# Weight splits issued ahead of other ready work on ScalarE and VectorE

## The chip, the cores and the metric

The kernel runs on one core of a Trainium2 chip. The metric is the device time of one execution in microseconds (us). Before the change the median of three runs is 1501.51 us (1500.48 to 1504.97).

## The reference, cut to what matters

A two-layer block (mixer A, convolutional FFN, mixer B, convolutional FFN, final norm) is followed by a block with a second mixer and a mixture of 32 experts. There are 256 tokens of width 1024, all in float32.

```python
for i in range(2):                       # first block
    x = x + (mixer_a if i == 0 else mixer_b)(rms_norm(x), ...)
    x = x + conv_ffn(rms_norm(x), ...)
h = rms_norm(x)                          # second block
proj = (rmsnorm(h) * (1 + sc1) + sh1) @ w_in          # 1024 -> q, kv, index, rwkv, 2 gates
o_attn = sparse_attention(q, k, v, index)             # 8 heads of 64
o_rwkv = rwkv7_time_mix(p_shift, ...)                 # 8 heads of 64, a recurrence over time
merged = sigmoid(gate_a) * (o_attn @ w_branch_attn) + sigmoid(gate_r) * (o_rwkv @ w_branch_rwkv)
h = h + gt1 * (merged @ w_out)
h = h + gt2 * moe(rmsnorm(h))            # top 2 of 32 experts, SwiGLU, 1024 -> 512 -> 1024
```

## The kernel before, in words

**Products of three.** Outside the experts every product of a weight matrix is made of three matmuls (`mm3`, L267 to L274): high part by high part (L272), and the two cross products (L273, L274). So each operand must be split in a high part in the fp32r format and a low part. `split_act` (L303 to L306) does it: ScalarE copies to the high part (L305), VectorE subtracts it from the source (L306). Activations are split by it too, and in other places by L366 (ScalarE) and L367 (VectorE) straight out of a transpose.

**The stream of weights.** `wload` (L244) takes a piece of 128 x 1024 weights: it issues the load on SyncE's queue (`load_raw`, L241) into a ring of raw places, and splits the piece into one of four split places, the tiles arena_r_78 to arena_r_81 in the orders below. A split place is free again when the last matmul that reads it is done, and a raw place when its split is done.

**Stages.** TensorE goes through mixer A, FFN, mixer B, FFN, final norms, the second mixer, the router, and the experts. In the second mixer the projections run first (`rwkv_prep` L967, `rwkv_pairs` L1038, `qkv` L1275, `gate` L1414). Eight gate groups of 48 matmuls each are spread over what follows. The RWKV recurrence (`rwkv_chain`, L1102) is a chain of small steps: it inverts a matrix (L1077 to L1087), writes it to memory and reads it back in another layout (L1090, L1128, both issued by ScalarE), and then goes through L1137, L1143, L1145, L1153, L1157 four times, and through L1167, L1173, L1178, L1187 four times. Between any two of these matmuls ScalarE or VectorE evacuates the result. After it comes `rwkv_out` (L1194, a group norm, transposes L1209, and a split). The attention goes in four parts: scores L1344, softmax on VectorE and ScalarE (L1346 to L1359), transposes L1364, product with the values L1370, split. `branch` (L1421) then multiplies attention by w_branch_attn and RWKV by w_branch_rwkv, and `second_mixer` (L1433) ends with w_out. In the orders below, pg_8110 to pg_9223 are the gates, pg_9291 to pg_9369 the attention branch, and pg_9410 and pg_9439 the RWKV branch.

**Experts.** `expert_pass` (L1668) streams 32 experts of 6 MB through places of 1 MB, loaded at L1665 on SyncE's queue. Twenty places are loaded ahead while the second mixer runs; every other load waits until a place is read by an expert matmul (L1709, L1735).

**What sets the order.** The program is handed to a scheduler that orders the instructions of each engine. Among instructions that it takes as ready it picks by priority, which without a mark is the place in the program. The engines then run their instructions in the order written, each waiting for its semaphores.

Of the kernel before, what the change touches and what calls it, by code (L numbers as in the profile page):

```python
# [90 lines left out]
def view(v, dims, dtype):  # L91
    if dtype not in (F32, F32R):
        v = v.bitcast(dtype)
    names = "abcde"[:len(dims)]
    if len(dims) > 1:
        left = f"({' '.join(names)})"
        v = v.rearrange(f"p {left} -> p {' '.join(names)}", **dict(zip(names, dims)))
    return v
# [8 lines left out]
class Net:  # L107
# [108 lines left out]
        return t  # L216


    PIECE, WPIECE = 1024, 2048

    def ring(self, raw, split):

# [21 lines left out]
    def wload(self, src):  # L244

        a, b = src.shape[1], src.shape[2]
        step = self.PIECE // b
        assert -(-a // step) <= len(self.places["split"][0])
        out = []
        for a0 in range(0, a, step):  # L250
            m = min(step, a - a0)
            raw = self.load_raw(src[:, a0:a0 + m])
            o = self.place("split")
            parts = [view(self.ar.cols(o + i * self.PIECE, m * b), (m, b), F32R) for i in range(2)]
            self.split_act(parts[0], parts[1], raw)
            out += [(parts[0][:, i], parts[1][:, i]) for i in range(m)]
        return out

# [1528 lines left out]
```

## Time and profile before

| what | before |
|---|---|
| median of 3 runs | 1501.51 us |
| the profiled execution | 1502.12 us |
| its span, first to last instruction | 1500.4 us |
| mean granted TensorE clock | 0.950 |
| TensorE busy | 1371.2 us |
| VectorE busy | 852.7 us |
| ScalarE busy | 615.2 us |

The span leaves 1.7 us of the profiled execution outside it, and the profiled execution lies 0.6 us over the median. A time in the rows is counted from the span's start. A matmul's duration is modelled and overlaps with the next one; the distance from start to start tells the pace.

### The profile page before, as it was taken

The page shows a single profiled execution, that of the slowest core. Times are in us where ns is not written, and L with a number is a line of the kernel's source. Part 1 is how long each engine was busy: PE and PEld are TensorE (multiplying, and loading weights), DVE is VectorE, ACT ScalarE, POOL GpSimd, SP SyncE. Part 2 cuts the span into 40 slices and gives each one's busy share as a digit, 9 for nine tenths or more (in the row PEclk, how much of TensorE's full clock was granted, in tenths as well). Part 3 has the DMA queues.
Part 4 walks back from the last instruction along what each step waited for, and adds up shares of the span by engine and source line. Part 5 has one row for each costly group of instructions (what it writes and reads, how often), then busy time and mean ns, then how long its engine had stood idle before and what let it go on. Part 6 is the DMA issues. An engine that isn't in the chain of part 4 may idle for free.

```text
span 1500.4 us, 22885 instructions
## 1 busy us (share of the span) xinstructions
PE 1371.2 (91%) x9085; PEld 1042.1 (69%) x9085; DVE 852.7 (57%) x1628; ACT 615.2 (41%) x955; POOL 32.2 (2%) x63
## 2 busy tenths in 40 slices
PE   7999999999999899999999899998978878879785
PEld 6778999999998689999798688887413313234131
DVE  5796798778788789878859742775201101101011
ACT  6644555556688555555575544552100000000000
POOL 3000000000001000000000100001000000000000
PEclk9999999999999999999899795999999989999998
DMA  9898586555555578563243352487999999999997
GB/s 318 282 327 277 158 274 215 187 187 160 170 182 184 172 272 275 187 191 109 72 153 113 99 121 86 170 336 308 390 421 420 420 420 421 421 421 419 421 419 253
DMA packets 165573, 391.18 MB, mean 261 GB/s; under 512 B 19440, under 2 KB 101100, under 8 KB 141780
## 3 DMA queue, kind: packets, MB, share of 16 engines
q1 hardware_dynamic: 153124, 383.64, 70.2%
q10 hardware_dynamic: 11136, 4.53, 1.3%
q0 software_dynamic: 1200, 1.49, 0.4%
q8 instruction: 73, 1.20, 0.3%
q14 instruction: 40, 0.33, 0.1%
HBM read 386.19 MB, written 3.43 MB: 260 GB/s over the span
## 4 chain that ended last, share of the span: by engine, by line
PE 58%; DMA 29%; DVE 7%; ACT 4%; issue 2%; SPq 0%; POOL 0%; DVEq 0%; ACTq 0%
DMA arena<-expert_w_gate 12%; PE ps L272 9%; PE ps L273 9%; PE ps L274 9%; DMA arena_w<-expert_w_gate 7%; DMA arena_w<-expert_w_down 6%; PE pc L273 5%; PE pc L272 5%; PE pc L274 5%; DMA arena<-expert_w_down 3%; PE pg L272 2%; PE pg L274 2%; PE pg L273 2%; DVE arena_r L306 2%; ACT arena_r L305 1%
## 5 line engine op out<-in xcount | busy, mean ns | idle before, releaser
L305 ACT ACTIVATE arena_r<-arena 128x1024 fp32r<-128x1024 f32 (+2 forms) x330 | 328.9, 1008 | 287.1 <-PE ps L273 73.1
L306 DVE TENSOR_TENSOR arena_r<-arena,arena_r 128x1024 fp32r<-128x1024 f32 (+2 forms) x330 | 376.9, 1154 | 119.2 <-ACT arena_r L305 115.8
L272 PE MATMUL ps<-arena_r,arena_r 128*128 128x256 f32 (+2 forms) x1192 | 353.7, 297 | 1.0 <-DVE arena L818 1.0
L273 PE MATMUL ps<-arena_r,arena_r 128*128 128x256 f32 (+2 forms) x1192 | 352.9, 296 | 1.1 <-DVE arena_r L306 1.1
L274 PE MATMUL ps<-arena_r,arena_r 128*128 128x256 f32 (+2 forms) x1192 | 352.4, 296 | 0.6 <-DVE arena_r L306 0.6
L272 PEld LDWEIGHTS ps<-arena_r,arena_r 128*128 128x128 f32 (+1 forms) x1192 | 229.3, 192 | 10.4 <-issue 3.5
L273 PEld LDWEIGHTS ps<-arena_r,arena_r 128*128 128x128 f32 (+1 forms) x1192 | 229.2, 192 | 7.2 <-DVE arena_r L306 1.5
L274 PEld LDWEIGHTS ps<-arena_r,arena_r 128*128 128x128 f32 (+1 forms) x1192 | 229.2, 192 | 5.6 <-DVE arena_r L306 0.8
L1709 PE MATMUL pc<-arena 128*32 128x512 f32 x576 | 144.4, 672 | 34.1 <-DMA arena<-expert_w_up 18.9
L272 PE MATMUL pc<-arena_r,arena_r 128*128 128x512 f32 x344 | 136.0, 399 | 5.3 <-ACT arena_r L305 3.4
L273 PE MATMUL pc<-arena_r,arena_r 128*128 128x512 f32 x344 | 135.9, 395 | 0.4 <-DVE arena_r L306 0.4
L274 PE MATMUL pc<-arena_r,arena_r 128*128 128x512 f32 x344 | 134.2, 393 | 0.0
L1709 PE MATMUL pc<-arena_w,arena 128*32 128x512 f32 x448 | 117.4, 663 | 15.8 <-DMA arena_w<-expert_w_gate 9.8
L1716 DVE TENSOR_TENSOR arena<-arena,pc 128x512 f32<-128x512 f32 x8 | 5.5, 688 | 204.6 <-PE pc L1709 204.6
L1692 ACT ACTIVATE arena<-ps,mod_col,moe_g 128x128 f32<-128x128 f32 x32 | 14.7, 458 | 246.1 <-DVE arena L1694 246.1
L1709 PEld LDWEIGHTS pc<-arena 128*32 128x32 f32 x576 | 31.4, 120 | 99.1 <-issue 37.1
L272 PE MATMUL pg<-arena_r,arena_r 128*128 128x256 f32 (+1 forms) x312 | 95.0, 306 | 2.0 <-DVE arena L916 1.8
L273 PE MATMUL pg<-arena_r,arena_r 128*128 128x256 f32 (+1 forms) x312 | 94.7, 305 | 1.1 <-DVE arena_r L306 1.1
L274 PE MATMUL pg<-arena_r,arena_r 128*128 128x256 f32 (+1 forms) x312 | 95.1, 306 | 0.2 <-DVE arena_r L306 0.2
L521 DVE SCALAR_TENSOR_TENSOR arena<-arena 128x255 f32<-128x255 f32 (+2 forms) x228 | 94.4, 477 | 0.2
L1735 PE MATMUL pc<-arena 128*32 128x512 f32 (+2 forms) x320 | 74.7, 584 | 11.5 <-DMA arena<-expert_w_down 7.6
L272 PEld LDWEIGHTS pc<-arena_r,arena_r 128*128 128x128 f32 x344 | 65.2, 190 | 19.8 <-ACT arena_r L305 5.1
(451 smaller groups left out, 1688.2 us busy)
## 6 DMA issues: line engine op xcount, KB each, us to landing
arena<-f_w_up SPq DMA_DIRECT2D x96, 512.0 KB, 3.9
arena<-expert_w_gate SPq DMA_DIRECT2D x41, 1024.0 KB, 19.9
arena<-expert_w_down SPq DMA_DIRECT2D x34, 1024.0 KB, 19.9
arena_w<-expert_w_up SPq DMA_DIRECT2D x33, 1024.0 KB, 19.9
arena<-expert_w_up SPq DMA_DIRECT2D x31, 1024.0 KB, 19.9
arena_w<-expert_w_down SPq DMA_DIRECT2D x26, 1024.0 KB, 19.9
arena<-ada_w SPq DMA_DIRECT2D x48, 512.0 KB, 5.6
arena<-f_w_down SPq DMA_DIRECT2D x48, 512.0 KB, 4.2
```

The source lines that it names most:

```text
L272: nc.tensor.matmul(acc, ah, bh, start=first, stop=False, **kw)
L273: nc.tensor.matmul(acc, ah, bl, start=False, stop=False, **kw)
L274: nc.tensor.matmul(acc, al, bh, start=False, stop=last, **kw)
L305: self.nc.scalar.activation(hi, src, AF.Copy)
L306: self.nc.vector.tensor_tensor(lo, src, hi.bitcast(F32), ALU.subtract)
L521: nc.vector.scalar_tensor_tensor(o[:, i:], src[:, :S - i], w[k - 1 - i], o[:, i:], op0=ALU.mult, op1=ALU.add)
L1692: nc.scalar.activation(xg[:, k], ps[:, j], AF.Identity, scale=g, bias=sh)
L1709: nc.tensor.matmul(gu[i][es], xg[:, kk, es], ws[e][:, k], start=kk == 0, stop=kk == 7, skip_group_check=True)
L1716: tt(hd, hd, gu[1], ALU.mult)
L1735: nc.tensor.matmul(o[es], hT[:, k0 + k, es], ws[e][:, k, f0 - c0:f0 - c0 + n], start=k0 + k == 0, stop=k0 + k == 3, skip_group_check=True)
```

## The change

The weight split inside `wload` is put under a raised priority of 3000; the splits of activations that call `split_act` elsewhere stay as they were. Loads, sizes, places and results are the same.

```diff
-    PIECE, WPIECE = 1024, 2048
+    PIECE, WPIECE, URGENT = 1024, 2048, 3000
...
             parts = [view(self.ar.cols(o + i * self.PIECE, m * b), (m, b), F32R) for i in range(2)]
-            self.split_act(parts[0], parts[1], raw)
+            with self.tc.high_priority(self.URGENT):
+                self.split_act(parts[0], parts[1], raw)
             out += [(parts[0][:, i], parts[1][:, i]) for i in range(m)]
```

The orders of ScalarE, VectorE, TensorE and SyncE differ after it. In the changed file every line from L255 on has a number higher by one, so L305 is L306 there, L366 is L367, and so on; the texts use the numbers of before.

ScalarE at the start of the kernel, before. L366 writes the normalized activations of the first layer, L305 the weights.

```order
L305 ACTIVATE arena_r_79<-arena 128x1024
L305 ACTIVATE arena_r_80<-arena 128x1024
L366 ACTIVATE arena_r_76<-ps_95,g_a 128x256
L366 ACTIVATE arena_r_76<-ps_96,g_a 128x256
L305 ACTIVATE arena_r_81<-arena 128x1024
L366 ACTIVATE arena_r_76<-ps_119,g_a 128x256
L366 ACTIVATE arena_r_76<-ps_95,g_a 128x256
L366 ACTIVATE arena_r_76<-ps_120,g_a 128x256
L366 ACTIVATE arena_r_76<-ps_96,g_a 128x256
L366 ACTIVATE arena_r_76<-ps_119,g_a 128x256
L305 ACTIVATE arena_r_78<-arena 128x1024
```

The same place on ScalarE, now:

```order
L306 ACTIVATE arena_r_79<-arena 128x1024
L306 ACTIVATE arena_r_80<-arena 128x1024
L306 ACTIVATE arena_r_81<-arena 128x1024
L367 ACTIVATE arena_r_76<-ps_95,g_a 128x256
L367 ACTIVATE arena_r_76<-ps_96,g_a 128x256
L306 ACTIVATE arena_r_78<-arena 128x1024
L367 ACTIVATE arena_r_76<-ps_119,g_a 128x256
L367 ACTIVATE arena_r_76<-ps_120,g_a 128x256
L367 ACTIVATE arena_r_76<-ps_95,g_a 128x256
L335 ACTIVATE ps_193,ss_10_194<-arena 128x512
L306 ACTIVATE arena_r_79<-arena 128x1024
L367 ACTIVATE arena_r_76<-ps_96,g_a 128x256
```

The third weight piece now stands ahead of the first activations, and the fourth and fifth ahead of most of the rest.

TensorE in the second mixer, where the first of the chain's four rounds ends and the second runs, before. Small shapes are the chain, L1344 and L1364 the attention, pg_9055 the fifth gate group.

```order
L1153 MATMUL pc_8405<-arena 32x32 x8
L1157 MATMUL pc_8415<-arena 32x32 x8
L1137 MATMUL pc_8425<-arena 32x16 x16
L1143 MATMUL pc_8443<-arena 16x16 x16
L1145 MATMUL pc_8443<-arena 32x16 x8
L272 MATMUL pg_9055<-arena_r_76,arena_r_79 128x256
L273 MATMUL pg_9055<-arena_r_77,arena_r_79 128x256
L1153 MATMUL pc_8471<-arena 32x32 x8
L1364 MATMUL ps_8913<-ident,arena 128x128 x3
```

The same place on TensorE, now:

```order
L274 MATMUL pg_9111<-arena_r_77,arena_r_78 128x256
L275 MATMUL pg_9111<-arena_r_76,arena_r_78 128x256
L1154 MATMUL pc_8405<-arena 32x32 x8
L1158 MATMUL pc_8415<-arena 32x32 x8
L1138 MATMUL pc_8425<-arena 32x16 x16
L1144 MATMUL pc_8443<-arena 16x16 x16
L1146 MATMUL pc_8443<-arena 32x16 x8
L273 MATMUL pg_9167<-arena_r_76,arena_r_79 128x256
L274 MATMUL pg_9167<-arena_r_77,arena_r_79 128x256
```

Between the first round's L1145 and its L1153 there now stand the rest of gate group 9055 and the whole of 9111, and the filler inside the chain is group 9167, which stood behind the chain before. Over the whole chain, from the first L1137 to the last L1187, there are 98 of the products of three (single matmuls) before and 197 now; between the last L1187 and the first matmul of the RWKV branch there are 190 before and 72 now.

TensorE around the last L1187 (the chain's end), before:

```order
L272 MATMUL pg_9167<-arena_r_76,arena_r_79 128x256
L273 MATMUL pg_9167<-arena_r_77,arena_r_79 128x256
L1187 MATMUL pc_8780<-arena 64x64 x8
L274 MATMUL pg_9167<-arena_r_76,arena_r_79 128x256
L272 MATMUL pg_9167<-arena_r_76,arena_r_79 128x256
```

And now:

```order
L1188 MATMUL pc_8780<-arena 64x64 x8
L1210 MATMUL pc_8839<-ident,arena 128x128 x2
L1365 MATMUL ps_8995<-ident,arena 128x128
L1210 MATMUL pc_8839<-ident,arena 128x128
L1365 MATMUL ps_8995<-ident,arena 128x128 x2
L1365 MATMUL ps_9000<-ident,arena 128x128 x3
L1371 MATMUL ps_9005<-arena 64x128
L1345 MATMUL ps_9014<-arena 128x128
L1371 MATMUL ps_9005<-arena 64x128 x5
L1345 MATMUL ps_9015<-arena 128x128
L1345 MATMUL ps_9014<-arena 128x256
L1345 MATMUL ps_9015<-arena 128x256
```

What followed the chain before was 94 matmuls of the last two gate groups; now the transposes of `rwkv_out` and the third and fourth parts of the attention follow it directly, with 24 matmuls of the attention branch among them.

## Rows read from the trace of the kernel before

**Rows 1.** Busy time, windows of the span; columns are named in the answer's head.
```profile
0.00:1050.00 1050.00, 1010.07 (x7203) 904.28 (x7207) 792.12 (x1513) 594.37 (x911) 32.23 (x63) 0.96 0.61 199
90.00:420.00 330.00, 329.98 (x2208) 301.88 (x2208) 266.55 (x415) 189.18 (x259) 0.00 (x0) 1.00 0.66 212
1050.00:1495.00 445.00, 361.13 (x1890) 137.80 (x1882) 60.63 (x117) 20.88 (x44) 0.00 (x0) 0.94 1.00 408
```

**Rows 2.** Waits of SyncE's DMA queue, 1000 to 1060 us.
```profile
SPq L1665 <- PE pc L1709: 23.2, 3, 19.1
```

**Rows 3.** Timeline of TensorE where the experts begin; start, us, what.
```profile
1047.76 4.06 PE L1709 MATMUL pc<-arena 128*32 128x512 f32 x34
```

**Rows 4.** Waits of TensorE, 0 to 1050 us: total, times, longest us.
```profile
PE pc L272 <- ACT arena_r L305: 3.4, 2, 1.7
PE pg L273 <- DVE arena_r L306: 1.1, 1, 1.1
...
PE pg L274 <- DVE arena_r L306: 0.2, 1, 0.2
```

**Rows 5.** Timeline of TensorE, 486 to 496 us: the two waits for L305.
```profile
486.73 0.49 PE L272 MATMUL pc<-arena_r,arena_r 128*128 128x512 f32 x1 [1.71 <-ACT arena_r L305]
...
495.07 0.50 PE L272 MATMUL pc<-arena_r,arena_r 128*128 128x512 f32 x1 [1.67 <-ACT arena_r L305]
```

**Rows 6.** Timeline of ScalarE, the same stretch.
```profile
486.05 0.63 ACT L305 ACTIVATE arena_r<-arena 128x512 fp32r<-128x512 f32 x1 [0.68 <-DVE arena L643]
...
494.40 0.62 ACT L305 ACTIVATE arena_r<-arena 128x512 fp32r<-128x512 f32 x1
```

**Rows 7.** Timeline of ScalarE, start of the kernel.
```profile
10.40 1.06 ACT L305 ACTIVATE arena_r<-arena 128x1024 fp32r<-128x1024 f32 x1 [0.66 <-DMA arena<-a_w_in]
11.37 0.82 ACT L366 ACTIVATE arena_r<-ps,g_a 128x256 fp32r<-128x256 f32 x2
12.08 1.06 ACT L305 ACTIVATE arena_r<-arena 128x1024 fp32r<-128x1024 f32 x1
```

**Rows 8.** Timeline of TensorE, its first product.
```profile
11.87 0.79 PE L272 MATMUL pc<-arena_r,arena_r 128*128 128x512 f32 x1 [1.89 <-ACT arena_r L366]
```

**Rows 9.** Timeline of TensorE, the RWKV chain and what follows it.
```profile
891.34 0.68 PE L1137 MATMUL pc<-arena 32*32 32x16 f32 x32
...
897.24 0.90 PE L1157 MATMUL pc<-arena 32*32 32x32 f32 x13 [1.87 <-ACT arena L1154]
...
958.65 1.14 PE L1187 MATMUL pc<-arena 64*64 64x64 f32 x16
...
969.41 0.92 PE L1344 MATMUL ps<-arena 64*128 64x128 f32 x4
...
980.02 0.27 PE L1364 MATMUL ps<-ident,arena 128*128 128x128 f32 x1
...
991.76 0.28 PE L273 MATMUL pg<-arena_r,arena_r 128*128 128x256 f32 x1
991.88 0.28 PE L274 MATMUL pg<-arena_r,arena_r 128*128 128x256 f32 x1
```

**Rows 10.** Timeline of VectorE, split of the last attention part.
```profile
984.03 0.42 DVE L306 TENSOR_TENSOR arena_r<-ps,arena_r 128x256 fp32r<-128x256 f32 x1 [1.39 <-ACT arena_r L305]
```

**Rows 11.** Windows ahead of and in the chain; third number from the end: granted clock.
```profile
830.00:840.00 10.00, 5.94 (x33) 4.40 (x34) 9.77 (x16) 7.71 (x13) 0.00 (x0) 0.91 0.59 180
840.00:850.00 10.00, 8.58 (x50) 7.99 (x47) 7.37 (x22) 6.04 (x11) 3.45 (x6) 0.50 0.17 54
...
897.00:934.00 37.00, 36.15 (x483) 30.89 (x483) 10.47 (x17) 17.57 (x46) 0.00 (x0) 0.50 0.28 86
934.00:958.00 24.00, 24.00 (x315) 20.90 (x313) 12.79 (x24) 10.49 (x19) 0.00 (x0) 1.00 0.16 48
```

**Rows 12.** Timeline of ScalarE, between the two memory trips of the RWKV chain.
```profile
870.73 5.22 ACTq L1090 DMA_DIRECT2D x_img<-arena  x8
876.28 0.60 ACT L1419 ACTIVATE arena<-pg 128x512 f32<-128x512 f32 x1 [8.00 <-DMA x_img<-arena]
```

## The prediction

> **What bounds the kernel now.** The windows of busy time come first, because they show two regimes. Up to 1050 us TensorE is busy 1010.07 of 1050.00 us; in 90 to 420 us it is busy 329.98 of 330.00 us at full clock. From 1050 us on the DMA share is 1.00 at 408 GB/s while TensorE has 361.13 busy of 445.00 us [rows 1]. So the second regime is a fixed stream of expert weights. It begins when TensorE begins the experts: the loads made ahead have filled every place, and SyncE's queue waits up to 19.1 us for the first expert matmuls to free one [rows 2], which start at 1047.76 us [rows 3]. The end therefore follows this start one for one when it comes later. A start some us earlier passes on too, as long as the loads ahead are in. What the change is worth is TensorE's idle time, plus time lost to a half clock, before 1047.76 us. Idle time there is 1050.00 - 1010.07 = 39.9 us in all [rows 1].
>
> The second view is what ends TensorE's waits. The change can only shorten directly those that end on a weight split. On L305 there are two, 3.4 us together; on L306 there are five, from 1.1 down to 0.2 us, which make 3.4 us [rows 4]. That would be 6.8 us, but the two on L305 stand at 486.73 and 495.07 us [rows 5], and the ScalarE instructions that finish just ahead of them are 128x512 pieces at 486.05 and 494.40 us, the first itself waiting for the recurrence's product at L643 [rows 6]. Weight pieces are 128x1024. These two waits are for splits of activations, which the change does not mark. So the direct gain is between 0 and 3.4 us. I take 1.5 us, below the middle, since a split place is freed only by a matmul's end whatever the priority.
>
> **The start of the kernel, a loss.** Before, ScalarE splits the second weight piece at 10.40 us, then the first two activations at 11.37 us, and the third piece at 12.08 us [rows 7]. TensorE's first product starts at 11.87 us, released by these activations [rows 8]. Now the third piece stands ahead of them. ScalarE was not idle between 10.40 and 12.08 us, so the trace does not say when that piece has landed. If it is in by 11.37 us, the activations come one split, 0.97 us from start to start (11.37 - 10.40), later. If it lands at the pace of the second piece behind the first, it is in at about 12.08 us, and the activations follow at 13.05 us, 1.68 us later. The fourth and fifth pieces ahead of the remaining activations can add some tenths in the first columns. I take 1.7 us. TensorE has 0.02 us idle in 90 to 420 us [rows 1], so no later slack gives this back.
>
> [...]
>
> **The middle, nothing.** In mixer A and the FFNs the splits move ahead of evacuations by one instruction or so. At 90 to 420 us TensorE is saturated, and the accumulators are double buffered, so a delay of one split (about 1 us) is hidden. At the stage changes norms and recurrence steps swap places with splits. Each swap can cost or save about one split; with some three places this is 0, with 3 us to either side. If the cover is gone, each costs 1 us.
>
> **The second mixer, a loss.** The gates are the filler that TensorE had for the time in which it would otherwise wait. Marked splits bring gate weights forward, so their matmuls are placed earlier: 19 matmuls of group 9055 ahead of the chain's first L1137, and 197 instead of 98 products inside the chain. In full clock such a matmul takes 0.12 us from start to start (991.76 to 991.88) [rows 9].
>
> First, the chain's end. Before, the chain runs from 891.34 to 958.65 + 1.14 = 959.8 us [rows 9]. Now 19 + 99 = 118 matmuls come ahead of its end: 118 x 0.12 = 14.2 us. The filler now covers the wait of 1.87 us for L1154 [rows 9]. The new end is 959.8 + 14.2 - 1.9 = 972.1 us.
>
> Second, from there to the RWKV branch. Before, it is at 991.9 us [rows 9], 32.1 us after the chain, and TensorE is kept busy by 190 products. Now 72 are left, 8.6 us. The branch must wait for the attention's last part. Its scores were at 969.41 us (to 970.3) and its transposes L1364 at 980.02 us [rows 9], 9.7 us of softmax on VectorE and ScalarE; the split of its result ends at 984.03 + 0.42 = 984.45 us [rows 10], 4.4 us after the transposes began. Now: about 3 us of transposes and of the third part after the chain, then the scores, so scores done at +3.5 us, transposes at +13.2 us, the split at +17.6 us. Behind it stand 12 + 48 products of the attention branch, 7.2 us, and so the RWKV branch starts at +24.8 us, that is at 996.9 us. Against 991.9 us it is 5.0 us later. TensorE has filler for only some 6 of the 17.6 us.
>
> Third, the clock. [...] I take 0.4 us, since the gap is broken by the transposes and 12 products. The term is 5.0 + 0.4 = 5.4 us. Its bounds: if softmax, freed from the gate evacuations, is 5 us faster, and the chain keeps its pace, it is 0; if softmax shares VectorE with the group norm as it did before, and the products run at the lower clock, it is 12 us.
>
> **The sum.** Against the profiled execution: 1502.12 + 1.7 - 1.5 + 0 + 5.4 = 1507.7 us. That execution is 0.6 us over the median, so I forecast 1507.1 us.
>
> **The rivals.**
> *The order moves, the time does not.* The matmuls are the same number, and if TensorE always has something placed, only idle time can be gained or lost. For it: the idle time up to 1050 us is only 39.9 us, and the second mixer hides nearly all its latency. Against it: 72 products do not fill a wait of 17.6 us. The start's 1.7 us and the gain's 1.5 us cancel, which gives 1501.7 us.
>
> *Faster, by the clock in the chain.* From 897 to 934 us the granted clock is 0.50 [rows 11], while the chain's small matmuls have little between them. [...] These 37 us at the full clock would give back at most 18 us, and half of that is 9 us. Then 1507.1 - 9 = 1498.1 us, and with the direct gain in full (1.9 us more), 1496.2 us; I put the case at 1496 us. It decides at the chain's second to fourth rounds: if they run at 1.0, this case is there. Against it: between the second and fourth round the new order has only some 30 products, hardly more than before, so the clock has the same reason to fall.
> [...]
>
> *Slower, by splits blocking the chain.* Splits now stand between the DMA issues of L1090 and between the chain's evacuations on VectorE (L306 four times, then L1139). A split waits for a split place, a place for the gate matmuls on TensorE, and the chain's evacuation waits behind the split. If two of the eight rounds are held by one gate group each, 48 x 0.12 = 5.8 us, the chain ends some 10 us later still, and this gives 1517 us. For it: the 8.00 us for which ScalarE stood behind L1090 [rows 12]. Against it: where TensorE works on gates meanwhile, nothing is lost.
>
> **Chances.** The forecast 0.36, no change 0.27, faster by the clock 0.22, slower by blocking 0.15. A measurement of this kernel tells a difference of about 0.3%, 4.5 us, from none; so below 1497.0 us is faster and above 1506.0 us slower. Of the forecast's case 0.06 lies within that bound, of the case without change 0.24, and of the faster one 0.02. So: slower 0.30 + 0.15 = 0.45, same 0.32, faster 0.23. The forecast's own range is 1501 to 1513 us, from the second mixer's 0 to 12 us around its 5.4 with the direct gain against it. The range over the cases is 1493 to 1519 us.
>
> **What the changed profile would show.** The first product near 13.5 us rather than 11.87 us. The two waits at 486 and 495 us still there in some form. The last L1187 near 972 us, then a gap of 5 to 12 us on TensorE ended by the softmax of the last attention part, and the first product of the RWKV branch near 996 us. The first expert matmul at about 1053 us, and from there to the end the same length as before. The forecast is wrong if the clock stays at 1.0 in the chain, if TensorE is not idle after it, or if the expert stage begins at the same time as before.

## The result: 1.4% slower, and the profile after

The changed kernel takes 1523.94 us (median of 4 runs, 1519.77 to 1525.47) where the kernel before, beside it, takes 1501.14: a ratio of 1.0142 [1.0116, 1.0168], 22.8 us. Forecast were 1507.1 us and a range up to 1519 us. The direction was right, the size was four times too small, and the time lies outside the range. In the changed kernel every line from L255 on has a number one higher (the splits are L306 and L307).

Windows of busy time of the kernel after, as in [rows 1]:

```profile
0.00:1050.00 1050.00, 1001.50 (x7109) 897.54 (x7110) 787.39 (x1454) 598.65 (x904) 26.76 (x61) 0.95 0.60 193
1071.00:1495.00 424.00, 344.80 (x1780) 130.77 (x1768) 56.04 (x106) 20.80 (x44) 0.00 (x0) 0.94 1.01 417
```

TensorE has 48.5 us idle up to 1050 us, against 39.9. The expert stage is what it was, a stream with a DMA share of 1.0. It only begins later. TensorE's timeline at the places that the prediction named:

```profile
13.41 0.79 PE L273 MATMUL pc<-arena_r,arena_r 128*128 128x512 f32 x1 [3.28 <-ACT arena_r L367]
...
498.86 0.79 PE L273 MATMUL pc<-arena_r,arena_r 128*128 128x512 f32 x1 [4.47 <-ACT arena_r L306]
...
911.13 0.68 PE L1138 MATMUL pc<-arena 32*32 32x16 f32 x32
...
984.39 1.60 PE L1188 MATMUL pc<-arena 64*64 64x64 f32 x16 [0.53 <-DVE arena L1175]
...
1067.84 0.64 PE L1710 MATMUL pc<-arena 128*32 128x512 f32 x4
```

The first product is 1.54 us later than in [rows 8], the RWKV chain begins 19.8 us later than in [rows 9], and the first expert matmul is 20.08 us later than in [rows 3]. The last computing instruction of the expert stage is on VectorE, before and after:

```profile
1491.55 0.51 DVE L1744 TENSOR_TENSOR arena<-arena,ps 128x128 f32<-128x128 f32 x2 [0.58 <-PE ps L1743]
```

```profile
1511.61 0.51 DVE L1745 TENSOR_TENSOR arena<-arena,ps 128x128 f32<-128x128 f32 x2 [0.58 <-PE ps L1744]
```

It is 20.06 us later, one for one with the start of the experts. (The other 1.7 us of the difference in span lie behind this instruction; they do not follow the marks, since that stretch is also 2.0 to 2.3 us longer in three of the four kernels below that mark one part, and 0.7 us shorter in the fourth.) So the whole loss stands ahead of the experts. TensorE's waits there, in total us, times, and longest us, say which places to look at:

```profile
PE pc L273 <- ACT arena_r L306: 6.3, 2, 4.5
...
PE ps L388 <- DVE arena L491: 4.0, 2, 2.5
PE pc L1005 <- DVE arena L323: 4.0, 1, 4.0
PE pc L1065 <- ACT arena L1070: 3.8, 1, 3.8
```

The waits for weight splits went as foretold: on VectorE's half from 3.4 us [rows 4] to 0.5. In their place stand waits for what the marked splits overtook. The 6.3 us are still activation splits, which had 3.4 us before; the other three rows are evacuations and small steps that had cost 1.3 us or less each.

### The profile page after: what moved, and what is told of

The parts are those of the page before. It is cut to its first block, busy times and chain, and to the rows that moved or that the text cites. A ratio compares the mean times of both kernels' runs of the same rounds, so it can differ in the third digit from the quotient of the medians.

```text
span 1522.2 us, 22915 instructions
## 1 busy us (share of the span) xinstructions
PE 1375.8 (90%) x9085; PEld 1046.8 (69%) x9085; DVE 858.8 (56%) x1628; ACT 622.5 (41%) x957; POOL 32.4 (2%) x63
## 4 chain that ended last, share of the span: by engine, by line
PE 60%; DMA 29%; DVE 6%; ACT 3%; issue 2%; SPq 0%; POOL 0%; DVEq 0%; ACTq 0%
DMA arena<-expert_w_up 11%; PE ps L273 9%; PE ps L274 9%; PE ps L275 9%; DMA arena_w<-expert_w_up 8%; DMA arena<-expert_w_down 7%; PE pc L273 5%; PE pc L274 5%; PE pc L275 5%; DMA arena_w<-expert_w_down 3%; PE pg L273 2%; PE pg L274 2%; PE pg L275 2%; DVE arena_r L307 2%; ACT arena_r L306 1%
## 5 line engine op out<-in xcount | busy, mean ns | idle before, releaser
L307 DVE TENSOR_TENSOR arena_r<-arena,arena_r 128x1024 fp32r<-128x1024 f32 (+2 forms) x330 | 376.9, 1156 | 144.9 <-ACT arena_r L306 139.0
L306 ACT ACTIVATE arena_r<-arena 128x1024 fp32r<-128x1024 f32 (+2 forms) x330 | 329.4, 1008 | 304.8 <-PE ps L274 91.1
L273 PE MATMUL ps<-arena_r,arena_r 128*128 128x256 f32 (+2 forms) x1192 | 353.7, 297 | 2.1 <-ACT arena_r L1409 2.1
L274 PE MATMUL ps<-arena_r,arena_r 128*128 128x256 f32 (+1 forms) x1192 | 352.9, 296 | 1.1 <-DVE arena_r L368 1.1
L275 PE MATMUL ps<-arena_r,arena_r 128*128 128x256 f32 (+2 forms) x1192 | 352.3, 296 | 0.0
L273 PEld LDWEIGHTS ps<-arena_r,arena_r 128*128 128x128 f32 (+1 forms) x1192 | 229.4, 193 | 10.8 <-issue 2.7
L274 PEld LDWEIGHTS ps<-arena_r,arena_r 128*128 128x128 f32 x1192 | 229.4, 192 | 7.2 <-DVE arena_r L368 1.3
L275 PEld LDWEIGHTS ps<-arena_r,arena_r 128*128 128x128 f32 (+1 forms) x1192 | 229.4, 192 | 5.0
L273 PE MATMUL pc<-arena_r,arena_r 128*128 128x512 f32 x344 | 138.9, 405 | 9.7 <-ACT arena_r L306 6.3
L274 PE MATMUL pc<-arena_r,arena_r 128*128 128x512 f32 x344 | 137.6, 400 | 0.0
L275 PE MATMUL pc<-arena_r,arena_r 128*128 128x512 f32 x344 | 135.6, 399 | 0.1
L273 PE MATMUL pg<-arena_r,arena_r 128*128 128x256 f32 (+1 forms) x312 | 97.4, 314 | 2.4 <-DVE arena L917 1.7
L274 PE MATMUL pg<-arena_r,arena_r 128*128 128x256 f32 (+1 forms) x312 | 96.0, 308 | 0.1
L275 PE MATMUL pg<-arena_r,arena_r 128*128 128x256 f32 (+1 forms) x312 | 95.2, 307 | 0.5 <-DVE arena_r L307 0.5
L1736 PE MATMUL pc<-arena 128*32 128x512 f32 (+2 forms) x320 | 74.2, 572 | 13.9 <-DMA arena<-expert_w_down 9.9
## 6 DMA issues: line engine op xcount, KB each, us to landing
arena<-expert_w_gate SPq DMA_DIRECT2D x41, 1024.0 KB, 19.8
```

The source lines that it names most:

```text
L273: nc.tensor.matmul(acc, ah, bh, start=first, stop=False, **kw)
L274: nc.tensor.matmul(acc, ah, bl, start=False, stop=False, **kw)
L275: nc.tensor.matmul(acc, al, bh, start=False, stop=last, **kw)
L306: self.nc.scalar.activation(hi, src, AF.Copy)
L307: self.nc.vector.tensor_tensor(lo, src, hi.bitcast(F32), ALU.subtract)
L1736: nc.tensor.matmul(o[es], hT[:, k0 + k, es], ws[e][:, k, f0 - c0:f0 - c0 + n], start=k0 + k == 0, stop=k0 + k == 3, skip_group_check=True)
```

## The experiments

Each of the first four marks the splits of one part of the kernel alone, with this edit, where `hot` is True in that part and False elsewhere:

```
+            with (self.tc.high_priority(self.URGENT) if self.hot else nullcontext()):
-            self.split_act(parts[0], parts[1], raw)
+                self.split_act(parts[0], parts[1], raw)
```

Two theories stood against each other for the second mixer. By the theory of the overtaken steps (theory 1) the marked splits hold back the small steps of `rwkv_prep` on the way to the chain, and this delay is the loss. By the theory of the moved gates, the prediction's, the gate products leave the tail, that is the stretch between the chain's end and the RWKV branch. In the first four expectations "theory 1" says something else: that each part adds its own delay to the end, and the rival that later parts absorb it. The kernels below keep the line numbers of the kernel before.

**Mixer A alone** (`hot` in mixer A):

> Weight splits are marked in mixer A only. Theory 1 (each stage adds its own delay, and no later stage gives it back): the delay that the full change had at the end of mixer A, +4.9 us (first L354: 179.6 against 174.7), reaches the end: 1501.1 + 4.9 = 1506 us, with the first product at 13.4 us and the second L387 waits of about 2.5 us. Rival (delays before the last mixer are absorbed, only the second mixer sets the end): 1501 us, first expert matmul at 1047.8 us.

1509.90 us, ratio 1.005 [1.0031, 1.0068]: dearer than either theory's time; the delay is not absorbed.

**The two FFNs alone:**

> Weight splits are marked in the two FFNs only. Theory 1: the full change gained 1 to 1.5 us of delay across the first FFN and lost 2 to 3 us across the second, so the sum is about -1.5 us: 1499.6 us (1498 to 1502). Rival (delays are absorbed): 1501 us.

1505.18 us, 1.0016 [1.0006, 1.0025]: a miss for both; a gain or nothing was expected.

**Mixer B alone:**

> Weight splits are marked in mixer B only. Theory 1: +6 us, 1507 us, with one wait of some 4.5 us of an out-projection matmul for the split of the last recurrence near 490 us. Rival (absorbed): 1501 us.

1507.18 us, 1.0025 [1.0016, 1.0035], as theory 1 had it.

**The second mixer alone:**

> Weight splits are marked in the second mixer only. Theory 1: +9 to +10 us, 1510.5 us, first expert matmul near 1057.5 us. Rival (only this stage matters): +20 us, 1521 us, first expert matmul near 1068 us.

1513.36 us, 1.0063 [1.0043, 1.0083]; the first expert matmul is where theory 1 had it, 9.75 us late.

The table reads TensorE's timeline at the same landmarks in each, as us later than in before (an empty field was not compared):

| landmark (before, us) | after | A | FFNs | B | second |
|---|---|---|---|---|---|
| first product (11.87) | +1.5 | +1.5 | | | |
| mixer A's transposes L387 (84.16) | +4.4 | +3.5 | | | |
| mixer B's first L909 (504.03) | +12.8 | +5.7 | +3.7 | +6.3 | |
| second mixer's first L951 (754.22) | +12.0 | +4.5 | +0.6 | +5.5 | +2.4 |
| normalised keys L1004 (827.37) | +20.2 | | | | +11.0 |
| chain's first L1137 (891.34) | +19.8 | | | | +9.9 |
| chain's last L1187 (958.65) | +25.7 | | | | +15.9 |
| first expert matmul (1047.76) | +20.1 | +4.7 | +0.8 | +5.7 | +9.8 |

The four add up to 4.71 + 0.81 + 5.71 + 9.75 = 20.98 us, against 20.08 of all together. So at the experts the parts add. On the way something is given back: the kernel with the FFNs alone is 3.7 us late at L909 and 0.6 at L951. By the medians, each against before beside it, the parts are 7.4 + 2.6 + 4.6 + 10.8 = 25.4 us against 22.8, so they add to within some 3 us.

What happens in mixer A is seen on VectorE (start, us, what), in before and then in after:

```profile
81.17 1.22 DVE L306 TENSOR_TENSOR arena_r<-arena,arena_r 128x1024 fp32r<-128x1024 f32 x1
...
83.63 0.87 DVE L490 SCALAR_TENSOR_TENSOR arena<-ps,arena 128x256 f32<-128x256 f32 x2
84.42 1.23 DVE L306 TENSOR_TENSOR arena_r<-arena,arena_r 128x1024 fp32r<-128x1024 f32 x1
```

```profile
84.22 1.21 DVE L307 TENSOR_TENSOR arena_r<-arena,arena_r 128x1024 fp32r<-128x1024 f32 x1
...
86.84 1.21 DVE L307 TENSOR_TENSOR arena_r<-arena,arena_r 128x1024 fp32r<-128x1024 f32 x1
87.97 0.86 DVE L491 SCALAR_TENSOR_TENSOR arena<-ps,arena 128x256 f32<-128x256 f32 x2
```

The split that stood behind the evacuation now stands ahead of it, and TensorE's transposes wait 2.54 and 1.46 us for the evacuation (0.58 and 0.67 before). The two waits grow by 2.75 us together, not by the one us of a split; at this end of a stage TensorE has nothing else placed that is ready.

In mixer B it is ScalarE, in before and then in the kernel that marks this mixer alone:

```profile
475.83 0.85 ACT L621 ACTIVATE arena<-ps,arena 128x256 f32<-128x256 f32 x2
```

```profile
479.04 2.51 ACT L305 ACTIVATE arena_r<-arena 128x1024 fp32r<-128x1024 f32 x3
481.46 0.46 ACT L621 ACTIVATE arena<-ps,arena 128x256 f32<-128x256 f32 x1
481.82 1.05 ACT L305 ACTIVATE arena_r<-arena 128x1024 fp32r<-128x1024 f32 x1
482.77 1.19 ACT L621 ACTIVATE arena<-ps,arena 128x256 f32<-128x256 f32 x3
...
493.34 0.63 ACT L305 ACTIVATE arena_r<-arena 128x512 fp32r<-128x512 f32 x1 [0.23 <-DVE arena L643]
```

Four weight splits (128x1024) stand ahead of the last tanhs of L621, which begin at 482.77 us instead of 475.83, and with them ahead of the last recurrence. The first half of its product is split at 493.34 us; in before that was 486.05 us [rows 6]. TensorE's timeline shows what follows:

```profile
488.73 0.39 PE L272 MATMUL pc<-arena_r,arena_r 128*128 128x512 f32 x1
488.95 0.39 PE L273 MATMUL pc<-arena_r,arena_r 128*128 128x512 f32 x1
...
494.03 0.80 PE L272 MATMUL pc<-arena_r,arena_r 128*128 128x512 f32 x1 [4.46 <-ACT arena_r L305]
...
496.12 0.63 PE L273 MATMUL pc<-arena_r,arena_r 128*128 128x512 f32 x1
496.55 0.63 PE L274 MATMUL pc<-arena_r,arena_r 128*128 128x512 f32 x1
```

The wait of 1.71 us [rows 5] is 4.46 us now. And the products that follow it start 0.43 us apart instead of 0.22: in windows of 1.5 us the granted clock is 1.00 from 480.00 to 492.00 us, 0.56 in the next, and 0.50 from 493.50 to 498.00 us. So this wait is paid twice. The windows of mixer B's stretch give both parts; before, then mixer B alone:

```profile
375.00:560.00 185.00, 177.51 (x1245) 159.79 (x1244) 151.29 (x273) 125.67 (x184) 5.65 (x11) 0.97 0.60 194
```

```profile
375.00:560.00 185.00, 175.16 (x1209) 158.22 (x1210) 147.94 (x266) 127.12 (x186) 5.66 (x11) 0.95 0.60 184
```

Idle time rises from 7.5 to 9.8 us. Time at the lower level, 0.50 (twice the length times one less the granted clock, summed over short windows) rises from 10.2 to 17.0 us, and half of the 6.8 us more is lost: 2.3 + 3.4 = 5.7 us, and 5.71 us were measured. So close a match is luck. From the start to the first expert matmul, after has 52.4 us idle against 39.9 and 105.8 us of low clock against 88.7, which makes 12.5 + 8.5 = 21.0 us, where 20.08 were measured; over all the changed kernels here this sum lies within 2.5 us of the measured delay. It is used below.

**Mixer A, without marks on the weights loaded ahead of the first product** (`hot` False while the first chunk's pieces load, then True):

> As mark_mixer_a, but the first column chunk (the four pieces split while the first activations are normalized) is unmarked. Theory 1 (a marked split costs where it overtakes a small activation step that TensorE needs first): the first product is back at 11.9 us and the start's 1.5 us are gone, so about +3 us over before at the first expert matmul, 1505 us; the wait at L387 stays. Rival (the start alone is the cost in mixer A, the rest follows from it): +0, 1502 us.

The first product is at 11.77 us, so these splits are the start's loss, and L387 still waits 2.31 us, both as theory 1 had it. Its time is a miss: the whole is at +2.2 us by 779 us, at +5.25 at the experts, 1508.72 us, 1.004 [1.0023, 1.0056]. The last 3 us arose between 779 and 811 us, where this kernel has before's order; see the last section.

**Mixer B with the recurrence above the marked splits:**

```
-                y = recur(P - 1, *todo, 4 if P < 3 else 2) if P > 0 else None
+                with self.tc.high_priority(6000): y = recur(...) if P > 0 else None
```

> As mark_mixer_b, and the recurrence of mixer B (its ScalarE and VectorE steps and the split of its result) is raised above the weight splits (6000 against 3000). Theory 1: the wait of 4.5 us for the last recurrence's split goes, and the end is within 1.5 us of before, 1502 us. Rival (the wait comes from late weight pieces or table loads of ScalarE, not from what overtakes the recurrence): +5 us, 1507 us.

A miss for both: 1522.12 us, 1.0134 [1.0117, 1.0151], the dearest of the experiments. The timelines of ScalarE and TensorE:

```profile
490.32 0.61 ACT L305 ACTIVATE arena_r<-arena 128x512 fp32r<-128x512 f32 x1
490.99 0.50 PE L272 MATMUL ps<-arena_r,arena_r 128*128 128x256 f32 x2 [4.34 <-ACT arena_r L305]
...
512.84 0.63 ACT L305 ACTIVATE arena_r<-arena 128x512 fp32r<-128x512 f32 x1 [2.33 <-DVE arena L643]
513.52 0.79 PE L272 MATMUL pc<-arena_r,arena_r 128*128 128x512 f32 x1 [4.11 <-ACT arena_r L305]
```

Both splits are of activations (128x512), not of weights. The first is the input of the mixer's gates, now behind a raised step of an earlier recurrence (L636) and its table load, and the gates' matmuls wait 4.34 us for it. The second is a half of the last recurrence's product, split at 512.84 us (500.46 with the marks alone), so the wait that the raise was to remove is still there. ScalarE also loads its table 21 times here, against 17 before and 19 with the marks, at 1.28 us each.

**Mixer B without marks on its output projection** (`hot` False around `out_proj`):

> As mark_mixer_b, but the weights of mixer B's output projection are unmarked. Theory 1 (in mixer B the cost is the last recurrence overtaken by splits of the output weights that TensorE cannot use before it): the wait of 4.5 us near 494 us shrinks to the 1.7 us of before, first L909 at +2 us instead of +6.3, the end at +1.5 us, 1503.5 us. Rival (any mark in mixer B costs, by table loads and reorder of the earlier parts): first L909 at +5 us or more, 1507 us.

The long wait is gone (1.99 and 1.67 us for the two halves, 1.71 and 1.67 in before), but mixer B still ends 4.0 us later, with an extra wait of 1.44 us: 1505.82 us, 1.0022 [1.001, 1.0033], between the two expectations. At L951 the delay is 2.2 us against 5.5 with all of mixer B marked. So the output projection's splits are the long wait's cause, but only a part of this mixer's loss.

**The second mixer marked, with `rwkv_prep` above the marks:**

```
-                fe = self.rwkv_prep(p, zz, KR, KB, bon, k, v, sg, a)
+                with tc.high_priority(6000): fe = self.rwkv_prep(...)
```

> As mark_second, and the preparation of the RWKV step (rwkv_prep, its small VectorE and ScalarE steps and its few matmuls) is raised above the weight splits (6000 against 3000). Theory 1 (overtaken activation steps are the cost): L1004 comes no later than in before by more than 3 us and the first expert matmul is at +1 to +4 us, 1503 to 1506 us. Rival (the cost is the gate matmuls that the marked splits bring ahead of the chain): the gates are still ahead, +10 us, 1512 us.

1499.43 us (10 runs, 1495.63 to 1502.36), 0.9975 [0.9964, 0.9985]: 13.9 us less than without the edit, below both expectations, and the one version that beats both kernels, by 2.8 us against before. Its profiled execution is the slowest of the ten. What theory 1 holds back is on VectorE; the small steps of `rwkv_prep` from L999 to the first Newton round's end (L314 to L322) and the splits between them, before, then with the second mixer marked:

```profile
813.04 0.17 DVE L999 TENSOR_SCALAR arena<-pc 128x16 f32<-128x16 f32 x1 [0.48 <-PE pc L997]
...
813.53 1.22 DVE L306 TENSOR_TENSOR arena_r<-arena,arena_r 128x1024 fp32r<-128x1024 f32 x1
...
820.58 0.16 DVE L322 SCALAR_TENSOR_TENSOR arena<-arena 128x16 f32<-128x16 f32 x1
```

```profile
817.65 0.18 DVE L999 TENSOR_SCALAR arena<-pc 128x16 f32<-128x16 f32 x1 [0.63 <-PE pc L997]
817.74 1.21 DVE L306 TENSOR_TENSOR arena_r<-arena,arena_r 128x1024 fp32r<-128x1024 f32 x1
...
821.92 1.21 DVE L306 TENSOR_TENSOR arena_r<-arena,arena_r 128x1024 fp32r<-128x1024 f32 x1
...
824.59 1.23 DVE L306 TENSOR_TENSOR arena_r<-arena,arena_r 128x1024 fp32r<-128x1024 f32 x1 [0.33 <-ACT arena_r L305]
...
827.56 1.23 DVE L306 TENSOR_TENSOR arena_r<-arena,arena_r 128x1024 fp32r<-128x1024 f32 x1
...
829.78 0.17 DVE L322 SCALAR_TENSOR_TENSOR arena<-arena 128x16 f32<-128x16 f32 x1
```

Each step waits for the one before, and four splits of 1.2 us step in between where there was one: these steps take 12.1 us instead of 7.5. (The other 4.6 us by which they are late were lost before L999.) L1004, which needs the result, is 11.0 us late. With `rwkv_prep` on top it is 11.3 us early, which is first a matter of its place: 116 fewer products of three (13.9 us at 0.12) stand ahead of it on TensorE than in before. They then stand behind it, and the chain still begins 7.8 us later than in before. The gain is inside the chain: 64.3 us from the first L1137 to the last L1187's end, with 216 gate products, against 68.4 us with 98. The windows in the chain, marked and then with `rwkv_prep` on top:

```profile
910.00:925.00 15.00, 12.38 (x214) 10.88 (x212) 3.32 (x5) 9.82 (x28) 0.00 (x0) 0.75 0.41 124
925.00:945.00 20.00, 20.00 (x282) 17.27 (x281) 4.09 (x9) 8.25 (x26) 0.00 (x0) 0.59 0.17 54
```

```profile
910.00:925.00 15.00, 15.00 (x346) 13.07 (x345) 5.50 (x10) 10.72 (x31) 0.00 (x0) 1.00 0.42 142
925.00:945.00 20.00, 20.00 (x319) 17.28 (x312) 6.50 (x11) 11.65 (x29) 0.00 (x0) 1.00 0.09 29
```

The granted clock stays at 1.00 where before it was 0.50 for 37 us [rows 11] and where the marked kernel has 24.2 us of low clock, which begins behind 2.6 us idle.

**The same with no marks, only `rwkv_prep` on top**, then **marked with `rwkv_pairs` on top**, then **`rwkv_pairs` on top with no marks:**

> No weight split is marked; only rwkv_prep is raised, by 3000. Theory 1: VectorE's steps L314 to L322 end some us earlier than 826.96 us and TensorE's waits of 1.1, 2.4, 1.65 us between 825 and 840 us shrink: -2 to -5 us, 1498 to 1500 us. Rival (every move away from program order costs): +2 us or more.

> As second_prep_first, and rwkv_pairs is raised above the weight splits too. Theory 1 (the chain of small steps is what should go first): L1077 comes earlier than at 856.79 us by up to 10 us, the RWKV chain starts earlier, and the first expert matmul is at -1 to -6 us, 1495 to 1501 us. Rival (TensorE's total work is fixed, and raising more of the chain only moves its idle time): the same as second_prep_first, 1499 to 1502 us, or worse.

> No weight split is marked; rwkv_prep and rwkv_pairs are raised by 3000. It tells what of second_prep_pairs_first is the marked splits: if they help once the preparation goes first, this run is slower than that one by 3 us or more (as prep_only was slower than second_prep_first by 4.3 us at the first expert matmul); if not, the two are equal.

1508.42 us, 1.0043 [1.0029, 1.0057]; 1507.13 us (1497.80 to 1511.93), 1.0027 [1.0007, 1.0046]; 1518.49 us, 1.0111 [1.0088, 1.0135]. The first two are misses for theory 1. The raised steps do come early (L1004 14 us earlier in the first and third, with 122 fewer products ahead of it), and all of it is lost again by the chain's start (6.7, 9.9 and 15.5 us later than in before). To raise the steps of the chain is therefore not good in itself; it paid only together with the marked splits, and with the pairs raised too, these still save 11 us (1518.49 against 1507.13). What the raised pairs lose in the marked kernel, against `rwkv_prep` alone on top, is clock: its order has 139 gate products in the chain, not 216, and 37.5 us of low clock there, not 0. Between these two kernels the first expert matmul differs by 8.6 us, of which half of the added low time up to there is 8.5 and the added idle time 0.8. Why its order leaves fewer products in the chain was not looked into.

**Second mixer, only ScalarE's half of a split marked:**

```
+            with (...high_priority...): self.nc.scalar.activation(parts[0], raw, AF.Copy)
+            self.nc.vector.tensor_tensor(parts[1], raw, parts[0].bitcast(F32), ALU.subtract)
```

> As mark_second, but only the ScalarE half of a weight split is marked; the VectorE half keeps its place. Theory 1 (the cost is on VectorE, whose queue is full between 800 and 840 us and where the marked subtractions overtake the steps L314 to L322): L1004 at +0 to +3 us instead of +11, the first expert matmul at +0 to +4 us, 1502 to 1506 us. Rival (ScalarE's copies or the gate matmuls that move with them are the cost): +8 us or more, 1511 us.

1510.47 us, 1.0056 [1.0035, 1.0076]. At the experts +8.5 of the 9.8 us, as the rival had it, with L1004 at +4.5 and 202 gate products in the chain; so marks on VectorE's half are not needed for the loss. That speaks against theory 1 as the cause.

**Second mixer, marks on the gates' weights alone**, and **on all but the gates':**

```
-            self.feats([ps], self.w2(2888 + 1024 * i + 128 * f, 256), self.hT)
+            self.hot = True; self.feats(...); self.hot = False
```

> Only the weight splits of the eight gate groups are marked. In its order 194 products of three stand inside the RWKV chain (98 in before, 197 in the full change). The prediction's own mechanism (the filler spent inside the chain is missing behind it) expects its +5 us, 1507.5 us, with a gap of some 10 us on TensorE behind the last L1187. The rival, theory 1 (overtaken steps of the RWKV preparation, which lies ahead of the gates), expects +0 to +2 us, 1503.5 us, and no such gap.

> All weight splits of the second mixer are marked but those of the gates; 117 products stand inside the chain. Theory 1: most of mark_second's +9.8 us is here, first L1004 at +9 us or more, the first expert matmul at +7 to +10 us, 1510.5 us. The prediction's own mechanism: +1 us, 1503.5 us.

1510.89 us, 1.0054 [1.0034, 1.0074], and 1503.66 us, 1.0011 [1.0001, 1.0021]. At the experts +7.1 and -0.5 us. Without marked gates L1004 is still 7.1 us late, but the last L1187 is 2.3 us late and the experts on time: that delay is given back. Part by part, as time beyond that of the products that moved (0.12 us each), the two kernels agree up to the chain's end: both lose 5.6 us ahead of the chain and win 5.5 in it. They differ in the tail alone: +7.3 us with marked gates, -1.1 without. Theory 1 falls as the cause of the end's loss; the moved gates make it, with 194 products in the chain against 117, and 94 in the tail against 171. The gap behind the chain is smaller than expected: 5.6 us idle from 971.5 to 999.5 us, in several pieces, not some 10.

**All marks, with `rwkv_prep` on top:**

> The full change, with rwkv_prep raised above the weight splits (6000 against 3000). Theory 1 with stages that add: the full change's +20.1 us at the first expert matmul less the 10.7 us between mark_second and second_prep_first, so +9.4 us (8 to 12), 1512.5 us. Rival (the delays of the full change are not those of its parts): above +16 us, 1519 us.

1507.78 us (1504.32 to 1516.19), 1.0034 [1.0019, 1.0049]: 16 us off the changed kernel, and 4.9 us above before, less than expected. In its profiled execution, the slowest of the ten, the first L951 is 18.0 us late and the first expert matmul 12.0. So there one line takes back the second mixer's loss and more, and what is left arose ahead of the second mixer.

## Why the prediction was wrong, step by step

- **The frame held.** The end follows the first expert matmul one for one: +20.08 there, +20.06 at the last instruction.
- **The start held.** Forecast 1.7 us and a first product near 13.5; measured 1.54 and 13.41, with the third piece now ahead of the activations. On ScalarE of after, as in [rows 7]:

```profile
10.57 1.06 ACT L306 ACTIVATE arena_r<-arena 128x1024 fp32r<-128x1024 f32 x1 [0.58 <-DMA arena<-a_w_in]
11.94 1.06 ACT L306 ACTIVATE arena_r<-arena 128x1024 fp32r<-128x1024 f32 x1 [0.31 <-DMA arena<-a_w_in]
12.90 0.82 ACT L367 ACTIVATE arena_r<-ps,g_a 128x256 fp32r<-128x256 f32 x2
```

  ScalarE stands 0.31 us before the piece, with the activations behind it, so the upper bound (1.68 us) was the nearer one.
- **The direct gain held as waits and was lost as time.** The five waits for VectorE's splits lost 2.9 of their 3.4 us. The two for activation splits, rightly set aside, grew by 2.9 us.
- **"The middle, nothing" failed.** Its value was 0, with 3 us to either side. Measured: mixer A 4.7 - 1.5 = 3.2, the FFNs 0.8, mixer B 5.7, together 9.7 us. The step priced a swap at one split and let gains and losses cancel. Three things were wrong. The swaps were not of both signs: every marked split moves forward, so an evacuation or recurrence step only moves back. Several splits stand ahead of one step (four in mixer B). And the clock was left out: half of the time at a granted clock of 0.50 comes on top of the idle time (in mixer B alone 6.8 us more of it, so 3.4 us). That 90 to 420 us is saturated [rows 1] was read as cover; it was no cover where TensorE had no other product ready, and the losses seen came where a stage ends (in after 2.54 us of wait at mixer A's L387, 4.47 us at mixer B's end).
- **The second mixer: the right mechanism, the wrong parts.** The sum, in the kernel that marks it alone, as time beyond that of the products that moved (0.12 us each; 19 into the stretch ahead of the chain, 99 into the chain, 118 out of the tail):

| part | forecast | measured |
|---|---|---|
| ahead of the chain | 0 | 9.9 - 2.3 = +7.6 |
| in the chain | -1.9 | (74.6 - 68.4) - 11.9 = -5.7 |
| tail to the RWKV branch | +6.9 and 0.4 for the clock | (25.0 - 32.2) + 14.2 = +7.0 |
| first product of the RWKV branch | +5.4 | +8.8 (1000.78 against 992.00) |

  The tail has the forecast size with other contents, so the size is in part luck. Its window in before, then in the kernel that marks the second mixer alone:

```profile
960.00:991.50 31.50, 30.57 (x238) 27.45 (x238) 21.90 (x58) 18.21 (x43) 0.00 (x0) 1.00 0.83 306
```

```profile
976.00:1001.00 25.00, 21.67 (x125) 17.34 (x124) 16.34 (x46) 11.79 (x29) 0.00 (x0) 0.74 0.79 302
```

  TensorE is idle for 3.3 us, not 11. The 0.4 us that the sum has for the lower clock was the author's estimate and no run shows it; in its place 6.5 us (half of 25 x 2 x 0.26) are lost to it here, at a granted clock of 0.74. The transposes and 12 products that were to break the gap ran in it, slowly. Ahead of the chain nothing had been forecast beyond the 19 products. The rival "faster, by the clock in the chain" came about in part: the low clock in the chain fell from 37.5 to 24.2 us, half of which is 6.7, and to nothing where `rwkv_prep` is raised. The forecast end of the chain, 972.1 us, was close in the second mixer alone (974.55 + 1.24) by luck, since a loss ahead of the chain that was not forecast and a larger gain in it nearly cancel; in after it is 984.39 + 1.60, with what came from upstream.
- **What the sum missed**, between the profiled executions, is 22.0 - 5.6 = 16.4 us: 9.7 in the middle (net of any gain), 1.5 of gain that was taken off beside it, 4.4 in the second mixer (9.75 against 5.4), less 0.2 at the start, make 15.4. With 1.7 us behind the last computing instruction, and less the 0.9 us by which the parts sum to more than the whole, it is 16.2. The rival "splits blocking the chain" had the nearest time, 1517 us, by luck, since it had not the place: the chain took less time for its products than before.

Open are why the order with raised pairs leaves fewer products in the chain, the 2.2 us of mixer B that its output projection does not explain, what makes the 5.6 us ahead of the chain in the kernel with the gates' marks alone, and the exact price of the kernel without marked gates, where idle and clock give +2.0 us at the experts and -0.5 was measured.

## What to carry to other kernels

A mark that moves prefetch-like work forward moves everything else on that engine back (in mixer B the last tanhs by 6.94 us); list the small steps that it now overtakes at each stage's end, where TensorE has nothing else ready, before counting the waits that it removes. Price a new wait on TensorE with the low clock that can stand behind it (in mixer B alone 4.46 us of wait, then 0.50 up to 498.00 us), and add stages up: losses upstream of a saturated stretch were given back only in small part (12.8 us at mixer B's end, 12.0 at the second mixer's start). Marking a part at a time and reading the same landmarks in every timeline showed in four runs where the loss was.

## What the runs showed that was not expected

Kernels with the same wait have different stretches of low clock behind it. At mixer A's L387 TensorE waits 2.54 us in after and 2.54 us in the kernel with mixer A alone. The windows there, after and then mixer A alone:

```profile
86.00:96.00 10.00, 6.00 (x31) 4.81 (x31) 9.51 (x17) 3.08 (x5) 0.00 (x0) 1.00 0.97 333
```

```profile
86.00:96.00 10.00, 7.35 (x24) 5.59 (x25) 9.14 (x15) 1.20 (x2) 0.00 (x0) 0.66 0.94 333
```

The first has no low clock (and 4.0 us idle), the second has 6.8 us of it. The kernel with all marks and `rwkv_prep` on top, whose marks are the same here, has 13.7 us up to 180 us, and its single executions lie 12 us apart. Likewise two kernels with edits in one mixer alone (mixer A without marks on the weights loaded ahead, mixer B without marks on its output projection) lost 3 us more between 779 and 811 us, in an order that was before's. The windows, before and then the first of the two:

```profile
779.00:811.00 32.00, 28.81 (x228) 26.72 (x228) 27.54 (x77) 20.33 (x41) 0.00 (x0) 0.95 0.43 134
```

```profile
779.00:811.00 32.00, 28.85 (x203) 26.52 (x202) 24.93 (x68) 19.23 (x40) 0.00 (x0) 0.84 0.45 122
```

The idle time is the same, 3.2 us; the difference is low clock, 10.2 us against 3.4. So a single profile of this kernel tells a stage's cost to some 3 us only.
